# A fixed TensorE order around each layer norm in a ten-phase transformer kernel

## The chip, the cores and the metric

One core of a Trainium2 chip runs the whole program. The metric is device time in microseconds (us) from one launch; the runs shown are three, with their median.

## The reference

The input is 256 tokens of 1024 features in float32. Two blocks follow each other. What matters here is how a phase ends:

```python
# first block, i = 0, 1: windowed attention (i = 0) or a gated linear recurrence (i = 1), then an MLP
x = layer_norm(DN_ALPHA * x + (1.0 + gate) * y, ln_g[i, 0], ln_b[i, 0])
y = sq_relu_mlp(x * (1.0 + scale) + shift, mlp_w1[i], mlp_w2[i])
x = layer_norm(DN_ALPHA * x + (1.0 + gate) * y, ln_g[i, 1], ln_b[i, 1])
# second block, i = 0, 1: gated feed-forward, mixer (attention and a gated delta rule), gated feed-forward
x = layernorm(DN_ALPHA_2 * x + 0.5 * swiglu(x, ffn_w13[i, 0], ffn_w2[i, 0]), ln_g[i, 0], ln_b[i, 0])
x = layernorm(DN_ALPHA_2 * x + hybrid_mixer(x, ...), ln_g[i, 1], ln_b[i, 1])
x = layernorm(DN_ALPHA_2 * x + 0.5 * swiglu(x, ffn_w13[i, 1], ffn_w2[i, 1]), ln_g[i, 2], ln_b[i, 2])
```

Each layer norm takes a token's mean and variance over 1024 features and gives (x - mean) / sqrt(variance + 1e-5), times a row, plus a row. `shift`, `scale` and `gate` come from a small product with a condition vector. There are ten phases and so ten norms: attn, mlp0, rnn, mlp1, ffn00, mix0, ffn01, ffn10, mix1, ffn11.

## The kernel before

**Products.** All weights stream through SBUF once, as tiles of 128 x 1024, in the order of their use. `get` (L336) issues the loads on SyncE's queue and splits each tile exactly into a high part (`hi`, ScalarE, L356) and a low part (`lo`, VectorE, L360; in quarters of 256 columns around a norm). A product then takes three matmuls: hi with the input's high part, hi with its low part, lo with the high part (L384 to L386 for a projection up, L402 to L404 in `mv_mm` for a projection down). The residual X lies as two tiles, `X[0]` and `X[1]`, a half of the tokens (128) each over 1024 features. The next phase's input is wanted transposed, features down the partitions: `hT`, with a high part (ScalarE, L373) and a low part (VectorE, L375).

**The end of a phase.** A projection down accumulates in four PSUM banks, `acc[half, c]`, for two halves of the tokens and two halves of the columns. The last four weight tiles (`LAG`, the tail) are left to `finish` (L614), which goes through them a half of the tokens at a time: for each half and column half, four tiles with three matmuls each, 24 matmuls for a half of the tokens. Then `ln_stats` (L554) makes the half's norm: VectorE multiplies by the gate's row where there is one (L562), adds the residual (L565), makes statistics of each column half (L567) and joins them (L569); GpSimd adds the epsilon (L570) and takes the power -1/2 (L571). Where the next phase's input isn't modulated (`direct`: mlp1 and the six phases after it), VectorE applies mean and row (L574, twice) and the power and row (L576, twice). Elsewhere (attn, mlp0, rnn) VectorE makes one factor (L578) and ScalarE applies both (L580, twice), and the rows wait until the transpose.

**The next phase's first products.** `turn` (L582) transposes a half: TensorE makes eight transposes of 128 x 128 in two groups of four, one group per column half of X (L589), into two PSUM banks of the `acc` kind. The result is copied to `h32`, by two copies of ScalarE where the norm is direct (L591), else by eight instructions with the features' scale and shift, ScalarE and VectorE in turns (L598, L596). `head_mm` (L605) makes the products of the next phase's first three weight tiles (four for mlp0, rnn and mlp1) in plain float32 from `h32`, for that half alone: eight products a tile, each two instructions of TensorE in the trace (L612). `turn_split` (L601) makes the high and low part of `hT` for the half.

**What sets the order.** The kernel is written in a framework that gives each engine its list of instructions before the run: it goes through the program with simulated times, and on each engine takes among the instructions that are ready then the one that was written first, or one marked with a high priority (as `turn` is). TensorE's list at a norm so follows from those simulated times: transposes can come between down products, and head products in another order than the loops'. On the chip each engine works its list in order.

The tail of the attention phase is the output projection of its last four heads, 4 to 7. `ph_attn` (L664) interleaves the heads' scores, probabilities and values with these products; each head's values become a tile `tT` that the down product needs.

## Time and profile before

| | us |
|---|---|
| three runs | 2159.17, 2160.49, 2160.00 |
| median | 2160.0 |
| span of the profiled execution | 2157.3 |
| TensorE busy in it | 2074.2 |
| VectorE busy | 1496.5 |
| ScalarE busy | 1056.3 |
| GpSimd busy | 152.2 |

The span goes from the first to the last instruction of the one execution that the profiler took; a run's time also has what lies around it. PE is TensorE's matmul side, PEld its loading of stationary operands, DVE VectorE, ACT ScalarE, POOL GpSimd, SP SyncE. A line such as L404 is a line of the kernel. Matmuls overlap, and the end of one is modelled, so the start of the next tells more than the end. In brackets stand the idle time of an engine before an instruction, and what ended it.

### The profile page before, as it was taken

The page shows a single profiled execution, that of the slowest core. Times are in us where ns is not written, and L with a number is a line of the kernel's source. Part 1 is how long each engine was busy: PE and PEld are TensorE (multiplying, and loading weights), DVE is VectorE, ACT ScalarE, POOL GpSimd, SP SyncE. Part 2 cuts the span into 40 slices and gives each one's busy share as a digit, 9 for nine tenths or more (in the row PEclk, how much of TensorE's full clock was granted, in tenths as well). Part 3 has the DMA queues.
Part 4 walks back from the last instruction along what each step waited for, and adds up shares of the span by engine and source line. Part 5 has one row for each costly group of instructions (what it writes and reads, how often), then busy time and mean ns, then how long its engine had stood idle before and what let it go on. Part 6 is the DMA issues. An engine that isn't in the chain of part 4 may idle for free.

```text
span 2157.3 us, 36524 instructions
## 1 busy us (share of the span) xinstructions
PE 2074.2 (96%) x14806; PEld 1903.0 (88%) x14806; DVE 1496.5 (69%) x2522; ACT 1056.3 (49%) x1798; POOL 152.2 (7%) x178
## 2 busy tenths in 40 slices
PE   4879999999999999999999999999999999999997
PEld 4769999898898999988999899999999889998997
DVE  5788979987656655788966655565569886666555
ACT  2444445784444444466634444444436664444442
POOL 1110000001000000011011100000001100100000
PEclk9899999999999999999999999999999999999999
DMA  9758974454664655454424455555535433355552
GB/s 323 274 225 325 345 293 174 173 198 177 234 236 155 223 193 179 154 189 149 145 79 177 159 221 194 179 193 179 192 139 209 139 133 137 108 198 184 186 186 79
DMA packets 67832, 411.80 MB, mean 191 GB/s; under 512 B 8304, under 2 KB 8480, under 8 KB 26960
## 3 DMA queue, kind: packets, MB, share of 16 engines
q1 hardware_dynamic: 59904, 384.85, 48.9%
q0 software_dynamic: 7616, 24.45, 3.6%
q8 instruction: 116, 1.90, 0.4%
q14 instruction: 52, 0.43, 0.1%
q10 hardware_dynamic: 144, 0.18, 0.0%
HBM read 408.35 MB, written 4.24 MB: 191 GB/s over the span
## 4 chain that ended last, share of the span: by engine, by line
PE 77%; DVE 12%; ACT 5%; DMA 3%; issue 2%; POOL 2%; POOLq 0%; DVEq 0%; SPq 0%; ACTq 0%
PE pu L384 13%; PE pu L386 13%; PE pu L385 13%; PE acc L402 6%; PE acc L403 6%; PE acc L404 6%; PE hd L612 3%; DVE lo L360 3%; PE py L386 2%; PE py L384 1%; PE py L385 1%; ACT hi L356 1%; DMA raw<-wst 1%; DMA aw<-ada 1%; DVE X L565 1%
## 5 line engine op out<-in xcount | busy, mean ns | idle before, releaser
L360 DVE TENSOR_TENSOR lo<-raw,hi 128x1024 fp32r<-128x1024 f32 (+1 forms) x689 | 730.2, 1068 | 415.6 <-ACT hi L356 407.0
L356 ACT ACTIVATE hi<-raw 128x1024 fp32r<-128x1024 f32 x574 | 605.7, 1058 | 710.1 <-PE pu L385 350.5
L384 PE MATMUL pu<-hT,hi 128*128 128x256 f32 x2672 | 765.3, 286 | 0.0
L386 PE MATMUL pu<-hT,lo 128*128 128x256 f32 x2672 | 758.2, 284 | 2.4 <-DVE lo L360 2.4
L385 PE MATMUL pu<-hT,hi 128*128 128x256 f32 x2672 | 758.2, 284 | 0.0
L384 PEld LDWEIGHTS pu<-hT,hi 128*128 128x128 f32 x2672 | 512.1, 192 | 18.0 <-issue 10.9
L385 PEld LDWEIGHTS pu<-hT,hi 128*128 128x128 f32 x2672 | 512.1, 192 | 5.7 <-issue 0.3
L386 PEld LDWEIGHTS pu<-hT,lo 128*128 128x128 f32 x2672 | 511.9, 192 | 5.1 <-DVE lo L360 2.6
L402 PE MATMUL acc<-hi,tT 128*128 128x512 f32 x688 | 270.0, 395 | 2.6 <-ACT tT L373 2.5
L403 PE MATMUL acc<-hi,tT 128*128 128x512 f32 x688 | 270.5, 393 | 0.7 <-DVE tT L375 0.6
L404 PE MATMUL acc<-lo,tT 128*128 128x512 f32 x688 | 270.2, 393 | 0.0
L404 PEld LDWEIGHTS acc<-lo,tT 128*128 128x128 f32 x688 | 129.3, 188 | 28.0 <-DVE lo L360 0.4
L402 PEld LDWEIGHTS acc<-hi,tT 128*128 128x128 f32 x688 | 129.4, 188 | 27.5 <-ACT tT L373 3.6
L403 PEld LDWEIGHTS acc<-hi,tT 128*128 128x128 f32 x688 | 129.5, 188 | 24.5 <-DVE tT L375 1.9
L612 PE MATMUL hd<-h,raw 128*128 128x128 f32 x960 | 113.0, 277 | 0.1
L612 PEld LDWEIGHTS hd<-h,raw 128*128 128x128 f32 x960 | 110.6, 193 | 2.4 <-ACT h L591 1.5
L452 DVE SCALAR_TENSOR_TENSOR aacc<-aw,csil,aacc 128x1024 f32<-128x1024 f32 x70 | 89.5, 1278 | 1.7 <-DMA aw<-adaw 1.4
L570 POOL TENSOR_SCALAR mv<-mv 128x1 f32<-128x1 f32 x20 | 12.1, 607 | 1100.5 <-DVE mv L569 1100.5
L373 ACT ACTIVATE tT<-r 128x256 fp32r<-128x256 f32 x152 | 61.5, 405 | 39.9 <-DVE r L782 28.0
L807 DVE SCALAR_TENSOR_TENSOR r<-r,pu 128x256 f32<-128x256 f32 x84 | 35.4, 422 | 64.5 <-PE pu L386 64.4
L375 DVE TENSOR_TENSOR tT<-r,tT 128x256 fp32r<-128x256 f32 x152 | 64.1, 422 | 4.8 <-ACT tT L373 4.8
L1007 DVE SCALAR_TENSOR_TENSOR cv<-pu,cl,cv 128x255 f32<-128x255 f32 (+2 forms) x144 | 66.7, 472 | 0.3
(368 smaller groups left out, 2590.7 us busy)
## 6 DMA issues: line engine op xcount, KB each, us to landing
raw<-wst SPq DMA_DIRECT2D x318, 1024.0 KB, 4.9
aw<-adaw SPq DMA_DIRECT2D x80, 512.0 KB, 6.0
aw<-ada SPq DMA_DIRECT2D x16, 512.0 KB, 5.6
bias<-bias_d POOLq DMA_DIRECT2D x32, 192.0 KB, 2.7
g<-rows POOLq DMA_DIRECT2D x10, 512.0 KB, 4.2
b<-rows POOLq DMA_DIRECT2D x10, 512.0 KB, 5.2
bias_d<-ext_d POOLq DMA_DIRECT2D x1, 2048.0 KB, 18.9
gbc<-g_d POOLq DMA_DIRECT2D x4, 512.0 KB, 5.4
```

Source lines behind the costliest of these rows:

```text
L356: S.activation(out=hi[:, 0:n], in_=r, func=AF.Copy)
L360: V.tensor_tensor(out=lo[:, c:c + m], in0=r[:, c:c + m], in1=hi[:, c:c + m].bitcast(F32), op=ALU.subtract)
L375: (eng or V).tensor_tensor(out=dlo, in0=src, in1=dhi.bitcast(F32), op=ALU.subtract)
L384: T.matmul(ps, lhsT=hi[:, c], rhs=r[:, 0:256], start=kk == 0, stop=False)
L385: T.matmul(ps, lhsT=hi[:, c], rhs=r[:, 256:512], start=False, stop=False)
L386: T.matmul(ps, lhsT=lo[:, c], rhs=r[:, 0:256], start=False, stop=kk == KT - 1)
L402: T.matmul(ps, lhsT=th, rhs=hi, start=first, stop=False)
L403: T.matmul(ps, lhsT=tl, rhs=hi, start=False, stop=False)
L404: T.matmul(ps, lhsT=th, rhs=lo, start=False, stop=last)
L452: V.scalar_tensor_tensor(out=acc, in0=w, scalar=csil[:, k:k + 1], in1=acc, op0=ALU.mult, op1=ALU.add)
L612: T.matmul(ps[:, half * 128:half * 128 + 128], lhsT=w[:, kk * 128:kk * 128 + 128], rhs=h32[:, kk, :], start=kk == 0, stop=kk == KT - 1)
L1007: V.scalar_tensor_tensor(out=o[:, n:256], in0=ps[:, 0:256 - n], scalar=wc(3 - n), in1=o[:, n:256], op0=ALU.mult, op1=ALU.add)
```

## The change

Four things change, all in how a phase ends.

1. In `ln_stats` the epsilon is added by VectorE instead of GpSimd, and the function returns its last VectorE instruction of the half.
2. `finish` gives TensorE's instructions in a fixed order, that in which they are written (`manual_schedule` for TensorE alone; the other engines' lists are made as before). The order is: the first half's 24 down products; of the second half's eight units (a column half and a tile, three matmuls each) six, `n + 2`; the first half's eight transposes; the last two units; the first half's head products up to five before their end; the second half's transposes; the last five; the second half's head products. The last norm has no next phase, and only the order of its down products is fixed.
3. `head_mm` takes the place at which it calls for the transposes, and goes through tile after tile, with all eight products of a tile.
4. VectorE's part of the first half's `turn_split`, the low part of `hT`, is queued behind the last VectorE instruction of the second half's norm (`issue_after`).

Comments and docstrings are also taken out, which does nothing.

```diff
@@ -567,20 +567,21 @@
             V.bn_stats(out=stt[:, c, :], in_=X[half][:, s])
         mv = pool.tile([128, 3], F32, tag="mv", bufs=2, name="mv")
         V.bn_aggr(out=mv[:, 0:2], in_=stt)
-        G.tensor_scalar(out=mv[:, 1:2], in0=mv[:, 1:2], scalar1=1.0, scalar2=LN_EPS, op0=ALU.mult, op1=ALU.add)
+        V.tensor_scalar(out=mv[:, 1:2], in0=mv[:, 1:2], scalar1=LN_EPS, scalar2=None, op0=ALU.add)
         G.tensor_tensor(out=mv[:, 2:3], in0=mv[:, 1:2], in1=mhalf[:, 0:1], op=ALU.pow)
         if last:
             for s in cs_:
                 V.scalar_tensor_tensor(out=X[half][:, s], in0=X[half][:, s], scalar=mv[:, 0:1], in1=ln["g"][:, s], op0=ALU.subtract, op1=ALU.mult)
             for s in cs_:
-                V.scalar_tensor_tensor(out=X[half][:, s], in0=X[half][:, s], scalar=mv[:, 2:3], in1=ln["b"][:, s], op0=ALU.mult, op1=ALU.add)
-            return
-        V.scalar_tensor_tensor(out=mv[:, 1:2], in0=mv[:, 0:1], scalar=-1.0, in1=mv[:, 2:3], op0=ALU.mult, op1=ALU.mult)
+                ins = V.scalar_tensor_tensor(out=X[half][:, s], in0=X[half][:, s], scalar=mv[:, 2:3], in1=ln["b"][:, s], op0=ALU.mult, op1=ALU.add)
+            return ins
+        ins = V.scalar_tensor_tensor(out=mv[:, 1:2], in0=mv[:, 0:1], scalar=-1.0, in1=mv[:, 2:3], op0=ALU.mult, op1=ALU.mult)
         for s in cs_:
             S.activation(out=X[half][:, s], in_=X[half][:, s], func=AF.Identity, scale=mv[:, 2:3], bias=mv[:, 1:2])
+        return ins
 
     def turn(half):
-        """transpose a half of the normalised tokens, then the scale and shift of its features"""
+
         h32 = per.tile([128, KT, 128], F32, tag="b4", bufs=4, name="h32")
         for kq in range(2):
             pt = ps_acc("pt")
@@ -602,33 +603,54 @@
         h32 = state["h32", half]
         split(hT[:, :, half * 128:half * 128 + 128], hT[:, :, 256 + half * 128:384 + half * 128], h32)
 
-    def head_mm(half, keys, hps):
-        for n, key in enumerate(keys):
+    def head_mm(half, keys, hps, at=None, then=None):
+
+        n = 0
+        for key in keys:
             if half == 0:
                 hps[key] = (get(*key), ps_up("hd"))
             w, ps = hps[key]
-            h32 = state["h32", half]
             for kk in range(KT):
-                T.matmul(ps[:, half * 128:half * 128 + 128], lhsT=w[:, kk * 128:kk * 128 + 128], rhs=h32[:, kk, :], start=kk == 0, stop=kk == KT - 1)
+                if n == at:
+                    then()
+                n += 1
+                T.matmul(ps[:, half * 128:half * 128 + 128], lhsT=w[:, kk * 128:kk * 128 + 128], rhs=state["h32", half][:, kk, :],
+                         start=kk == 0, stop=kk == KT - 1)
 
     def finish(acc, tail, nxt):
-        """the last down products, a half of the tokens at a time, the norm, and the next phase's first products"""
+
+
         n = len(tail)
         keys = [(nxt,) + it for it in items_of(nxt)[:nf(nxt)]] if nxt else []
         hps = {}
         if nxt:
             hT = per.tile([128, KT, 512], F32R, tag="hT", bufs=1, name="hT")
-        for half in range(2):
-            for c in range(2):
-                for j, (t, (hi, lo)) in enumerate(tail):
-                    mv_mm(acc[half, c], t, half, hi[:, c * 512:c * 512 + 512], lo[:, c * 512:c * 512 + 512], False, j == n - 1)
-            ln_stats(half, acc, ln["direct"])
+
+        def turn_(half):
+            with tc.high_priority():
+                turn(half)
+
+        def down(half, units):
+            for c, j in units:
+                t, (hi, lo) = tail[j]
+                mv_mm(acc[half, c], t, half, hi[:, c * 512:c * 512 + 512], lo[:, c * 512:c * 512 + 512], False, j == n - 1)
+
+        units = [(c, j) for c in range(2) for j in range(n)]
+        with tc.manual_schedule(engines={mybir.EngineType.PE}):
+            down(0, units)
+            ln_stats(0, acc, ln["direct"])
+            down(1, units[:n + 2])
+            if nxt:
+                turn_(0)
+            down(1, units[n + 2:])
+            ins = ln_stats(1, acc, ln["direct"])
+            if nxt:
+                head_mm(0, keys, hps, 8 * len(keys) - 5, lambda: turn_(1))
+                with tc.issue_after(ins.ins):
+                    turn_split(0, hT)
+                head_mm(1, keys, hps)
+                turn_split(1, hT)
         if nxt:
-            for half in range(2):
-                with tc.high_priority():
-                    turn(half)
-                head_mm(half, keys, hps)
-                turn_split(half, hT)
             for key in keys:
                 head[key] = hps[key][1][:, 0:256]
             state["hT"] = hT
@@ -640,7 +662,7 @@
         ln["es"].close()
```

## Rows read from the trace of the kernel before

**Rows 1.** The page's first part: each engine's busy time in the span.
```profile
PE 2074.2 (96%) x14806; PEld 1903.0 (88%) x14806; DVE 1496.5 (69%) x2522; ACT 1056.3 (49%) x1798; POOL 152.2 (7%) x178
```
**Rows 2.** Waits of PE at the transposes: us in total, times, longest us.
```profile
PE pt L589 <- ACT X L580: 7.5, 5, 5.3
PE pt L589 <- DVE X L576: 6.3, 12, 0.6
```
**Rows 3.** Timeline of PE, end of ffn00 (start, us, engine, line, operation [idle before]).
```profile
890.29 0.39 PE L402 MATMUL acc<-hi,tT 128*128 128x512 f32 x1
890.52 0.39 PE L403 MATMUL acc<-hi,tT 128*128 128x512 f32 x1
891.47 0.66 PE L589 MATMUL pt<-cs,X 128*128 128x128 f32 x4 [0.56 <-DVE X L576]
```
**Rows 4.** Down products behind the transposes: stretch, PE busy (count); mlp0, rnn, mlp1, ffn00.
```profile
343.70:344.85 1.15, 0.92 (x3) 1.00 0.00 0
512.80:513.45 0.65, 0.38 (x1) 1.00 0.00 0
700.70:701.20 0.50, 0.50 (x2) 1.00 0.00 0
891.95:894.02 2.07, 1.88 (x7) 1.00 0.00 0
```
**Rows 5.** Timeline of DVE and POOL, end of ffn00, first half's norm.
```profile
887.09 0.69 DVE L565 SCALAR_TENSOR_TENSOR X<-X,acc 128x512 f32<-128x512 f32 x1 [0.28 <-PE acc L404]
...
888.54 0.21 DVE L569 BATCH_NORM_AGGREGATE mv<-stt 128x2 f32<-128x12 f32 x1
888.79 1.41 DVE L574 SCALAR_TENSOR_TENSOR X<-X,mv,g 128x512 f32<-128x512 f32 x2
890.66 1.42 DVE L576 SCALAR_TENSOR_TENSOR X<-X,mv,b 128x512 f32<-128x512 f32 x2 [0.46 <-POOL mv L571]
...
889.67 0.95 POOL L571 TENSOR_TENSOR mv<-mv,mhalf 128x1 f32<-128x1 f32 x1
```
**Rows 6.** The epsilon on POOL, all norms: duration ns min/median/max, first and last start.
```profile
L570 POOL TENSOR_SCALAR mv<-mv x20: 183/742/1287, 147.6 to 2148.5; 128x1 f32<-128x1 f32 x20
```
**Rows 7.** Timeline of DVE and PE, end of ffn00, second half's norm.
```profile
895.77 1.21 DVE L375 TENSOR_TENSOR hT<-h,hT 128x1024 fp32r<-128x1024 f32 x1
...
899.89 0.63 PE L589 MATMUL pt<-cs,X 128*128 128x128 f32 x4 [0.56 <-DVE X L576]
...
901.21 0.60 PE L612 MATMUL hd<-h,raw 128*128 128x128 f32 x3
```
**Rows 8.** Timeline of PE, both halves' transposes at mlp0's, rnn's and mlp1's end.
```profile
343.21 0.66 PE L589 MATMUL pt<-cs,X 128*128 128x128 f32 x4 [0.46 <-ACT X L580]
...
352.66 1.36 PE L589 MATMUL pt<-cs,X 128*128 128x128 f32 x8 [0.45 <-ACT X L580]
...
512.30 0.65 PE L589 MATMUL pt<-cs,X 128*128 128x128 f32 x4 [0.79 <-ACT X L580]
...
518.72 0.66 PE L589 MATMUL pt<-cs,X 128*128 128x128 f32 x4 [0.49 <-ACT X L580]
...
699.58 1.32 PE L589 MATMUL pt<-cs,X 128*128 128x128 f32 x8 [0.37 <-DVE X L576]
...
707.23 1.38 PE L589 MATMUL pt<-cs,X 128*128 128x128 f32 x8 [0.50 <-DVE X L576]
```
**Rows 9.** Timeline of DVE, rnn's end: the last scaled features of the second half.
```profile
522.34 0.76 DVE L596 TENSOR_SCALAR h<-pt,ha,hb 128x128 f32<-128x128 f32 x2
```
**Rows 10.** Attention's norm: transposes; stretches with PE busy (count), granted clock, DMA share, GB/s.
```profile
149.55 1.97 PE L589 MATMUL pt<-cs,X 128*128 128x128 f32 x8 [5.31 <-ACT X L580]
...
141.15:144.25 3.10, 3.08 (x13) 1.00 0.95 390
149.50:153.00 3.50, 3.45 (x16) 0.50 0.00 0
153.00:167.60 14.60, 14.60 (x131) 1.00 0.68 247
```

## The prediction

> **What bounds the kernel now.** I read the page's first part: of the span's 2157.3 us TensorE is busy for 96% [rows 1]. So a change of TensorE's order can only win what TensorE idles away around the norms, and the waits of TensorE say how much that is: its transposes waited 7.5 us for ScalarE's normalised rows and 6.3 us for VectorE's, 17 waits in all [rows 2]. One of the 17 is 5.3 us, at the norm after the attention; the other 16 make 8.5 us. A wait is longer on TensorE's clock than the idle time shown: a product lasts 0.39 us but the next starts 0.23 us after it [rows 3], so each wait also loses the 0.16 us in which its predecessor drains. Outside the attention that is 8.5 + 16 × 0.16 = 11.1 us, half a per cent of the time: **the ceiling** of this change, but for the attention's norm and the last norm's end.
>
> The execution in the profile has a span of 2157.3 us; the median of the timed runs is 2160.0, 2.7 us more, which holds what lies around the span. I carry every sum over to the median. A measurement of this kernel can tell some 0.2%, 4.3 us, from no change.
>
> **Five plain norms (ends of ffn00, mix0, ffn01, ffn10, mix1).** I work one, ffn00's, and the others repeat its pattern.
>
> First half. The transposes start at 891.47, where the products before them would have let them start at 890.52 + 0.23: 0.72 us lost [rows 3]. Seven of the second half's 24 down products stood behind the transposes' start [rows 4], 17 ahead. The change puts 18 ahead (6 units of 3): nearly the order that there is. The extra product covers 0.23 us. The other help is the epsilon, which goes from GpSimd to VectorE. The chain on VectorE is residual sum 887.09, aggregate 888.54, L574 twice, then L576, which waits for GpSimd's power [rows 5]. The power ends at 889.67 + 0.95 = 890.62 and L576 starts 0.04 later, while L574 was done at 888.79 + 1.41 = 890.20. GpSimd's epsilon takes 0.74 us in the median and 0.18 at the least [rows 6]. On VectorE I take 0.2 us, by the aggregate's 0.21 us, the nearest row of a tiny VectorE instruction; bounds are 0.1 and 0.4. Then L574 ends at 890.4, the power before that, and L576 starts at 890.45 instead of 890.66: 0.2 us won. Against this, the four later transposes need the second column half of X, which comes 0.71 us (half of L576's 1.42) after the first, while four transposes take 0.45: 0.26 us of new wait, where before a down product filled it. First half: 0.23 + 0.2 − 0.26, **0.2 us won**.
>
> Second half. Its transposes start at 899.89 with 0.56 + 0.16 = 0.72 us lost; the head products behind them start at 901.21 [rows 7], 1.32 us after 899.89, which is 0.2 more than the ten instructions between (0.113 us each) need: 0.9 in all. In VectorE's chain stands the low part of the first half's input (L375), 1.21 us from 895.77 [rows 7]. The change holds it back behind the norm: 1.1 us off the chain (0.1 overlapped). With 0.2 for the epsilon and 0.2 for down products that end sooner, X is ready for TensorE at about 898.4. But TensorE's order moves too: the transposes come after 19 of 24 head products instead of 23. Head products start at about 893.8; one is two instructions of 0.113 us (131 instructions, eight of them transposes, in 14.6 us [rows 10]), so 19 take 4.3 us: TensorE is there at 898.1. That leaves 0.3 us of wait and 0.26 for the second column half, against 0.9: **0.35 us won**. The five products that are left (1.1 us) cover the copies. L375 itself costs nothing where it goes: VectorE has nothing from 900.4 but the next weights' low parts, and the low part is wanted only when the head products end, after 905. If that cover went, the price would be its 1.21 us.
>
> Five norms × (0.2 + 0.35) = **2.7 us won**.
>
> **Four norms with a gate.** Here the order does move, by the counts of [rows 4]: 3 products stood behind the transposes at mlp0's end, 1 at rnn's, 2 at mlp1's; now 6. So the transposes come up 3, 5 and 4 products sooner (0.7, 1.1 and 0.9 us) and X comes only 0.2 us sooner: first halves lose 0.5, 1.0 and 0.7 us, and rnn's another 0.3 for the second column half, which a product covered. Second halves lost 0.61 (mlp0), 0.65 (rnn) and 0.66 (mlp1) [rows 8], and 0.3 more between the two groups at mlp0 and mlp1 (eight transposes take 1.36 and 1.38 us where 1.06 would do). Without L375, mlp0's second half wins its 0.9 whole; mlp1's chain had no L375 in it, wins 0.1. At rnn I expect 0.15: fixed order runs a tile's eight head products through all features before the next tile, and the last of rnn's scaled features ended at 522.34 + 0.76 = 523.1, 4.4 us after its transposes began [rows 8, 9], where 5 products, 8 transposes and 7 products of a tile cover 3.6. Sum: mlp0 +0.4, rnn −1.15, mlp1 −0.6: **1.3 us lost**.
>
> The attention's norm. At 141.18 TensorE gets head 7's values and needs 12 more products in 3.1 us (13 instructions with the last of an earlier one) [rows 10]; the other tail products had filled gaps earlier. In fixed order (column half by column half, all four tiles in each), only three products each of heads 4, 5 and 6 can run early. So 39 products, 9.0 us, stand behind 141.2, 33 of them ahead of the transposes. They fill the hole of 5.31 us before 149.55 [rows 10] and the first half's sum starts later: its last columns come at about 145.7 (15 products, 0.4 to drain, and an estimated 0.6 for head 7's low part), 4.3 us of chain (887.09 to 891.47), transposes at 150.0 plus 0.3. Six products and the eight transposes later, at 152.6, the head products start, 1.3 us later than now. [...] I take **1.0 us lost**; bounds are 1.7 won (only the clock's gain counts) and 7.9 lost (the rival "attention").
>
> The last norm has no transposes; the epsilon saves its 0.2 us on the path to the end. No DMA is added or moved past; GpSimd's queue loses 20 short instructions. TensorE's other queue neighbours keep their place, since all that follows needs the new input.
>
> **Sum:** 2.7 − 1.3 − 1.0 + 0.2 = 0.6 us won. The framework will also order the other engines anew; no row prices that, and I add nothing for it to the sum (to the range some 2 us on either side). So 2160.0 − 0.6 = 2159.4 us.
>
> [...] The rows show that GpSimd and VectorE get into each other's way: 0.18 us alone, 0.74 beside L574 [rows 5, 6], and the power ended 0.43 us after the second L574. [...] But GpSimd's epsilon had ended before the power began at 889.67, while the second L574 ran until 890.20 [rows 5], so I take it that the power can slip in between the two as well. Otherwise it is the rival "port".
>
> **The rivals.**
> *Hidden* (faster): second halves wait no more, because VectorE's chain tightens by more than I allow once L375 is out. For it: L375 is the one long piece between stats and aggregate. Against: 4 products fewer are ahead of the transposes. It wins 0.55 more at five norms, 0.85 at mlp1, 0.5 at rnn: 4.1 us, so 2155.3, and with 1.0 at the attention, if the held clock pays for the delay there, 2154.3; its limit, all 11.1 us, is 2149.
> *Attention* (slower): TensorE, emptied of 27 tail products before 141.2, idles there as long as before 149.55, its clock falls to the 0.50 level in front of the 39 products, and 27 × 0.23 = 6.2 us plus 1.7 us at half clock stand uncovered. For it: the clock did fall once, after 5.31 us. Against: the scores and probabilities of heads 6 and 7 stay there to break the idle time, and the norm's own chain was waited out anyway. It decides where an idle stretch before 141.2 grows as long as that of 5.31 us. Instead of 1.0 lost, 7.9: 2159.4 + 6.9 = 2166.3.
> *Port*: at 13 chains (two halves of six norms with L574, the last) the power ends 0.43 us after both L574s: 0.17 us later than now instead of 0.2 sooner, 13 × 0.37 = 4.8: 2164.2.
> *Nothing moves*: the framework's order was 17 products against 18; if the fixed order is otherwise the same, only the epsilon counts, 0.2 us where the transposes wait for it and at the end, some 2 us: 2158.
>
> **How the numbers follow.** Forecast 0.48, hidden 0.25, attention 0.13, port 0.08, nothing moves 0.06. The forecast's own range is 2156 to 2162. The range goes from 2152 (into hidden, short of its limit) to 2164.5 (past port, short of attention), leaving out some 0.2. Faster than 2155.7 is hidden, 0.25; slower than 2164.3 is attention, 0.13; the rest, 0.62, is within 0.2%.
>
> **What would show it.** In the changed profile: the plain norms' transposes waiting some 0.3 us twice in each half; L375 of the first half behind L576; the power starting right after a VectorE epsilon, and ending before L574 (else port); rnn's and mlp1's first transposes waiting over 1.2 us; at the attention, no hole of 5 us and a granted clock of 1.00 to 155 us. Second halves with no wait mean hidden; a clock of 0.50 before 145 us means attention. The forecast is wrong if the head products end more than 3 us sooner or later against the norm's start than the sums say, or if the difference arises between norms.

## The result and the profile after

| | before | changed |
|---|---|---|
| timed runs, median (lowest to highest), us | 2159.59 (2158.43 to 2160.49) | 2170.4 (2168.54 to 2174.82) |
| span of the profiled execution, us | 2157.3 | 2167.8 |

The changed kernel is **slower**: the ratio of its runs to those of the kernel before is 1.0064, with a 95% interval of 1.005 to 1.0078. The prediction was 2159.4 us with a range of 2152 to 2164.5, so it was wrong. (The ratio on record is not the quotient of the two medians, which is 1.005.)

The page's first part, against [rows 1]:

```profile
PE 2083.8 (96%) x14806; PEld 1908.8 (88%) x14806; DVE 1499.8 (69%) x2542; ACT 1060.7 (49%) x1798; POOL 142.1 (7%) x158
```

TensorE has the same 14806 instructions and the same share of the span, but they take 9.6 us more. Most of that, 7.2 us, is at the attention's norm, where part of them ran at a lower clock (stretches below). Next TensorE's waits, in the columns of [rows 2] (us in total, times, longest us):

```profile
PE pt L590 <- ACT X L580: 10.5, 5, 3.5
...
PE pt L590 <- DVE X L576: 1.8, 2, 1.2
```

The transposes are now at L590. Their waits for VectorE's rows, at the direct norms, have nearly gone (12 waits and 6.3 us before, 2 and 1.8 now). Their waits for ScalarE's rows, at the three norms with scaled features, have grown from 7.5 to 10.5 us. The total at the transposes is even a little lower, 12.3 against 13.8, so this view alone doesn't explain 10 us.

What does is to ask where along the program the two executions come apart. I compared the start of the same product up (the k-th hi-times-high-part product in both traces) ahead of each norm and behind it. The table says how many us later each kernel is behind the norm than the kernel before, counted from ahead of it, in one profiled execution each. At the attention I count from the last instruction that stands at the same place in every kernel's list of TensorE (at 124.24 us in the kernel before). Up to there the lists are the same, and yet the other executions come there 2.7 to 5.8 us sooner: the kernel before was slow there in its profiled execution, which is no effect of any edit. The plain norms are five, summed. Kernels with the same edits at a norm differ there by up to 1.5 us (2 at e2's plain norms), so smaller differences between two cells say little.

| kernel | attn | mlp0 | rnn | mlp1 | plain norms | whole span |
|---|---|---|---|---|---|---|
| changed | +12.7 | +3.9 | +1.3 | +0.6 | −4.7 | +10.5 |
| e1, attention in the framework's order | +1.5 | +3.4 | +1.3 | +0.6 | −5.0 | −0.4 |
| e2, fixed at the plain norms only | +2.9 | +0.1 | −1.8 | −0.4 | −2.8 | −7.3 |
| e3, epsilon on GpSimd | +12.4 | +2.1 | +2.3 | +1.6 | +0.2 | +17.6 |
| e4, low part free | +13.6 | +2.9 | −0.3 | +3.3 | +0.1 | +13.6 |
| e5, attention tile by tile | +5.4 | +3.9 | +1.3 | +0.7 | −4.6 | +4.4 |
| e6, none left behind at mlp0, rnn | +11.3 | +1.3 | −0.4 | +0.6 | −5.2 | +1.6 |
| e7, next phase's work tied | +6.8 | +2.3 | −0.2 | +0.7 | −4.9 | +3.3 |
| e8, two VectorE edits, no order | +3.2 | −1.0 | −1.8 | −0.5 | −6.4 | −8.5 |
| e9, epsilon alone | +2.1 | +0.2 | −0.5 | −0.4 | −1.1 | −4.8 |
| e10, low part alone | +0.1 | +0.3 | −1.4 | −0.1 | +1.2 | +2.4 |
| e11, order mended | +0.8 | +2.8 | +3.4 | +0.6 | −5.0 | −1.6 |
| e12, e8 and next phase's work tied | +0.1 | −0.8 | −0.7 | −0.5 | −6.4 | −6.8 |

The rest of each span's difference lies ahead of the attention's norm, between norms (the framework also orders the other engines anew) and at the last norm. So the change won 4.7 us at the plain norms, and lost 18.5 at the four norms of the first block, 12.7 of it at the attention's. Together that is 13.8 us lost (the last norm, where 1.1 us are won, is not in the table); the ratio of 1.0064 is 13.8 us as well.

The attention's part as a whole, from the common instruction to the first product up behind the norm, before and then changed (stretch, PE busy (count), granted clock, DMA share, GB/s):

```profile
124.24:170.18 45.94, 38.48 (x243) 0.93 0.63 240
```

```profile
121.12:179.76 58.64, 45.65 (x243) 0.85 0.73 260
```

**The attention's norm.** First the kernel before, then the changed one, in stretches of 4 us (the changed execution is 3.1 us ahead at the common instruction):

```profile
132.00:136.00 4.00, 2.64 (x13) 1.00 0.60 240
136.00:140.00 4.00, 3.21 (x16) 1.00 0.29 51
140.00:144.00 4.00, 3.99 (x18) 1.00 0.96 396
```

```profile
132.00:136.00 4.00, 1.44 (x5) 1.00 0.01 2
136.00:140.00 4.00, 2.77 (x9) 0.75 0.83 275
140.00:144.00 4.00, 4.00 (x10) 0.50 0.98 397
144.00:148.00 4.00, 4.00 (x17) 0.89 0.69 249
```

Between 132 and 140 us TensorE ran 29 instructions before (28 in the 8 us that are the same place of the program), and 14 now; the down products that had filled the gaps stand, in their fixed order, behind products of heads whose values aren't there. Its granted clock falls to 0.50, at which ten products then run one behind the other. TensorE's timeline of the changed kernel (start, us, engine, line, operation [idle before]) shows what follows:

```profile
139.64 0.79 PE L402 MATMUL acc<-hi,tT 128*128 128x512 f32 x1 [0.47 <-ACT tT L373]
...
145.39 0.39 PE L404 MATMUL acc<-lo,tT 128*128 128x512 f32 x1
...
152.82 1.36 PE L590 MATMUL pt<-cs,X 128*128 128x128 f32 x8 [2.84 <-ACT X L580]
...
155.43 0.83 PE L617 MATMUL hd<-h,raw 128*128 128x128 f32 x6
...
165.95 1.97 PE L590 MATMUL pt<-cs,X 128*128 128x128 f32 x8 [3.47 <-ACT X L580]
...
179.76 0.28 PE L384 MATMUL pu<-hT,hi 128*128 128x256 f32 x1
```

The product at 145.39 is the first half's last. The first transposes come 3.3 us later than before [rows 10], 6.4 us later at the same place of the program, and the second ones wait a second time, 3.47 us. In the kernel before the second half's chain had begun in the one hole (at 146.69 us) and ended under the first head products, and its transposes came at 154.03 without a wait. At 165.95 the clock is low once more (0.61 from 165.95 to 169.50 us). The first product up, at 170.18 before, comes at 179.76.

VectorE's timeline shows what kept the second half. Its own links are L562, L565, L567, L569, L570 and L578:

```profile
157.04 0.68 DVE L562 TENSOR_TENSOR t<-acc,g 128x512 f32<-128x512 f32 x1
157.64 0.75 DVE L450 TENSOR_SCALAR aacc<-aw,csil 128x1024 f32<-128x1024 f32 x1
158.30 0.69 DVE L565 SCALAR_TENSOR_TENSOR X<-X,t 128x512 f32<-128x512 f32 x1
158.90 1.28 DVE L452 SCALAR_TENSOR_TENSOR aacc<-aw,csil,aacc 128x1024 f32<-128x1024 f32 x1
160.09 0.69 DVE L567 BATCH_NORM_STATS2 stt<-X 128x6 f32<-128x512 f32 x1
160.75 1.23 DVE L360 TENSOR_TENSOR lo<-raw,hi 128x1024 fp32r<-128x1024 f32 x1
161.89 0.20 DVE L569 BATCH_NORM_AGGREGATE mv<-stt 128x2 f32<-128x12 f32 x1
162.01 1.17 DVE L360 TENSOR_TENSOR lo<-raw,hi 128x1024 fp32r<-128x1024 f32 x1
163.10 0.15 DVE L570 TENSOR_SCALAR mv<-mv 128x1 f32<-128x1 f32 x1
163.16 1.28 DVE L452 SCALAR_TENSOR_TENSOR aacc<-aw,csil,aacc 128x1024 f32<-128x1024 f32 x1
164.89 0.16 DVE L578 SCALAR_TENSOR_TENSOR mv<-mv 128x1 f32<-128x1 f32 x1 [0.45 <-POOL mv L571]
```

VectorE is never idle but for the last 0.45 us, and yet the chain takes 8.0 us. The framework has put an instruction of the mlp0 phase into every gap of it: multiply-adds of the modulation (L450, L452) and full-width low parts of weights (L360). Where nothing is put into such a gap it is short (0.03 us between L569 and L570 at ffn00's norm, second half, in this kernel), and the work in it here is 0.75 to 1.28 us long.

### The profile page after: what moved, and what is told of

It is laid out like the page before. It is cut to its first block, busy times and chain, and to the rows that moved or that the text cites. A ratio compares the mean times of both kernels' runs of the same rounds, so it can differ in the third digit from the quotient of the medians.

```text
span 2167.8 us, 36514 instructions
## 1 busy us (share of the span) xinstructions
PE 2083.8 (96%) x14806; PEld 1908.8 (88%) x14806; DVE 1499.8 (69%) x2542; ACT 1060.7 (49%) x1798; POOL 142.1 (7%) x158
## 5 line engine op out<-in xcount | busy, mean ns | idle before, releaser
L360 DVE TENSOR_TENSOR lo<-raw,hi 128x1024 fp32r<-128x1024 f32 (+1 forms) x689 | 730.6, 1069 | 415.8 <-ACT hi L356 406.8
L571 POOL TENSOR_TENSOR mv<-mv,mhalf 128x1 f32<-128x1 f32 x20 | 19.4, 972 | 1121.0 <-DVE mv L570 1121.0
L452 DVE SCALAR_TENSOR_TENSOR aacc<-aw,csil,aacc 128x1024 f32<-128x1024 f32 x70 | 89.4, 1277 | 2.6 <-DMA aw<-adaw 2.3
L375 DVE TENSOR_TENSOR tT<-r,tT 128x256 fp32r<-128x256 f32 x152 | 64.1, 422 | 5.3 <-ACT tT L373 5.3
```

Source lines behind the costliest of these rows:

```text
L360: V.tensor_tensor(out=lo[:, c:c + m], in0=r[:, c:c + m], in1=hi[:, c:c + m].bitcast(F32), op=ALU.subtract)
L375: (eng or V).tensor_tensor(out=dlo, in0=src, in1=dhi.bitcast(F32), op=ALU.subtract)
L452: V.scalar_tensor_tensor(out=acc, in0=w, scalar=csil[:, k:k + 1], in1=acc, op0=ALU.mult, op1=ALU.add)
```

## Experiments

The kernel before ran beside each of them on the same chip, with medians between 2155 and 2157 us there, so what counts is the ratio; where an expectation is in microseconds, I set beside it the ratio times the 2159.6 us of the kernel before. (By that rule the changed kernel is at 2173.4, and not at the 2170.4 from which the expectations count.) In the expectations "the planner" is the part of the framework that makes the engines' lists, and P, S, E, L, H, F, B, T, P', O and F' are theories.

### Is it the place of the order, or something else?

```diff
 e1, e2: finish()
+        if ph not in FIXED:      # e1: all but attn; e2: the ffn and mixer phases
+            for half in range(2):
+                down(half, units)
+                ln_stats(half, acc, ln["direct"])
+            for half in range(2 if nxt else 0):
+                turn_(half)
+                head_mm(half, keys, hps)
+                turn_split(half, hT)
 e3: ln_stats()
-        V.tensor_scalar(out=mv[:, 1:2], in0=mv[:, 1:2], scalar1=LN_EPS, ...
+        G.tensor_scalar(out=mv[:, 1:2], in0=mv[:, 1:2], scalar1=1.0, scalar2=LN_EPS, ...
 e4: finish()
-                with tc.issue_after(ins.ins):
-                    turn_split(0, hT)
+                turn_split(0, hT)
```

> The changed kernel with the order at the attention norm alone left to the planner, as before the change; everything else as changed. Theory P (the fixed order pays at the plain norms and costs at the attention norm, where TensorE is held to products whose values are late, and at the norms of mlp0 and rnn): the 9.6 us by which the two traces come apart at the attention norm come back, 2160 to 2162 us, and TensorE waits for X before its first transposes about 5 us, not 6.3. Rival S (the losses come from the planner's other choices, that any edit stirs, not from the order at this norm): within 3 us of the changed kernel's 2170.4. Rival E (the epsilon on VectorE): no change either, 2170.

> The fixed order at the norms of the ffn and mixer phases and at the end alone (six of ten); at attn, mlp0, rnn and mlp1 the planner's order as before. Theory P: the five plain norms win 0.9 us each and the end 1.1, together about 5.7 on the kernel before, so 2153 to 2156 us, less than both kernels. Rival S: between 2159 and 2168, since the mixers' other work is stirred again. Rival E (epsilon on VectorE at all ten norms is what costs): 2165 to 2170.

> The changed kernel with the epsilon's addition back on GpSimd. Theory P: the order is the cause, the addition a small gain of the change, so 2170 to 2173 us. Rival E (one more step of VectorE's chain, ahead of which the planner sets other work of up to 1.3 us): some 3 to 8 us faster, 2162 to 2167.

> The changed kernel without the tie of the first low part to the second half's norm. Theory P: the tie is worth nothing much, 2168 to 2173 us. Rival L (the tie makes the first up products of the next phase late, by the low part's 1.3 us at each of nine norms): 2159 to 2165.

| | median, us | ratio to before | 95% interval |
|---|---|---|---|
| e1 | 2159.6 | 1.0016 | 1.0003 to 1.003 |
| e2 | 2151.95 | 0.9981 | 0.9965 to 0.9998 |
| e3 | 2174.73 | 1.0079 | 1.0059 to 1.0099 |
| e4 | 2177.55 | 1.0095 | 1.0076 to 1.0114 |

The order at the attention's norm alone costs 0.5% (1.0064 against 1.0016). (e1 also leaves the low part untied at this norm; e4, untied with the order kept, loses as much there as the changed kernel, so the tie is not the cause.) With the order taken away at mlp0, rnn and mlp1 too, the kernel is faster than before. Against the 2159.6 us that is 2163.1 and 2155.5: P's second number came, and its first was missed by 1 us; the first transposes of e1 wait 6.0 us, and not about 5. But only half of P holds: e3 and e4 say that the gain of the plain norms comes from somewhere else. Take either of the two edits of VectorE away, keep the whole order, and the plain norms win nothing (+0.2 and +0.1 in the table). E and L, by which these runs would have been faster, are ruled out by the times. That each of the two edits helps is seen in the table; by time, e3's interval overlaps widely with the changed kernel's and e4's barely. P had taken both edits for nearly free: 1.0079 and 1.0095 are 2176.7 and 2180.1 us, above its ranges.

(In e2 the plain norms win 2.8 us and not 4.7, because of ffn10's norm alone, which loses 1.2; its cause is told with e9 and e10.)

What the two edits do is seen in VectorE's timeline at ffn00's norm, second half. In the changed kernel:

```profile
908.75 0.68 DVE L565 SCALAR_TENSOR_TENSOR X<-X,acc 128x512 f32<-128x512 f32 x1
...
912.63 0.21 DVE L569 BATCH_NORM_AGGREGATE mv<-stt 128x2 f32<-128x12 f32 x1
912.87 0.15 DVE L570 TENSOR_SCALAR mv<-mv 128x1 f32<-128x1 f32 x1
912.94 1.41 DVE L574 SCALAR_TENSOR_TENSOR X<-X,mv,g 128x512 f32<-128x512 f32 x2
914.26 1.41 DVE L576 SCALAR_TENSOR_TENSOR X<-X,mv,b 128x512 f32<-128x512 f32 x2
915.59 1.22 DVE L375 TENSOR_TENSOR hT<-h,hT 128x1024 fp32r<-128x1024 f32 x1
```

With the epsilon on GpSimd (e3) L576 waits for the power, as before:

```profile
908.91 0.68 DVE L565 SCALAR_TENSOR_TENSOR X<-X,acc 128x512 f32<-128x512 f32 x1
...
914.90 1.41 DVE L576 SCALAR_TENSOR_TENSOR X<-X,mv,b 128x512 f32<-128x512 f32 x2 [0.44 <-POOL mv L571]
```

With the low part free (e4) it stands in the chain again, as in [rows 7]:

```profile
906.29 0.68 DVE L565 SCALAR_TENSOR_TENSOR X<-X,acc 128x512 f32<-128x512 f32 x1
...
910.06 1.21 DVE L375 TENSOR_TENSOR hT<-h,hT 128x1024 fp32r<-128x1024 f32 x1
...
912.81 1.41 DVE L576 SCALAR_TENSOR_TENSOR X<-X,mv,b 128x512 f32<-128x512 f32 x2
```

From the first L565 to the end of L576 that is 6.92 us in the changed kernel, 7.41 without the epsilon's move and 7.93 without the tie; in the kernel before, 8.42. The two steps, 0.5 and 1.0 us, simply add up.

### What loses at the first block's norms

e5 gives the attention's last products another fixed order, e6 leaves no products behind the first transposes at mlp0 and rnn, e7 keeps the next phase's VectorE work out of the attention's norm, and e8 has the two VectorE edits without any order.

```diff
 e5: finish(), for ph == "attn"
+                for half in range(2):
+                    down(half, [(c, j) for j in range(n - 2) for c in range(2)])
+                units = [(c, j) for j in range(n - 2, n) for c in range(2)]
             down(0, units)
             ln_stats(0, acc, ln["direct"])
-            down(1, units[:n + 2])
+            down(1, units[:2])
 e6: finish(), for mlp0 and rnn
-            down(1, units[:n + 2])
+            down(1, units)
             turn_(0)
-            down(1, units[n + 2:])
 e7: behind() is issue_after(the last VectorE instruction of the attention's norm) during mlp0
+                    with behind():
                         ada_mac(*seq[n - 3])
+                with behind() if m == n else ExitStack():
                     for c in range(0, n, m):
                         V.tensor_tensor(out=lo[:, c:c + m], ...
 e8: FIXED = (), and in the order as written
+                ins = ln_stats(half, acc, ln["direct"])
                 head_mm(half, keys, hps)
+                with tc.issue_after(ins.ins):
                     turn_split(half, hT)
```

> The changed kernel, with the last down products of the attention phase alone in another fixed order: both halves and both column halves of heads 4 and 5 first, then heads 6 and 7; the transposes have the same 6 products behind them. Theory H (at this norm the fixed order holds some 30 ready products behind head 7's values, so TensorE stands idle between 132 and 140 us at a falling clock, and the first half's last product ends at 147.2 us instead of about 143): 4 to 6 us faster than the changed kernel, 2164 to 2166, and the granted clock is 1.00 between 140 and 144 us. Rival F (the norm's links on VectorE set the end, with work of the next phase between them): within 2 us, 2168.5 to 2171.

> The changed kernel with the first transposes behind all of the second half's products at the norms of mlp0 and rnn (none left behind them, where the change leaves 6). Theory B (the transposes stand 1.8 and 2.1 us in front of 6 products that were ready): the waits shrink by the 6 x 0.233 = 1.4 us at each, 2 to 3 us faster, 2167 to 2168. Rival (the second half's chain, which starts 1.4 us earlier then, has its own wait of the same length later, or was late for another reason): 0 to 5 us faster, with the gain in the second transposes' wait too. Rival F (the chain of VectorE decides, not the place of the transposes): within 1 us of 2170.

> The changed kernel; VectorE's work of the mlp0 phase that needs no norm (the modulation's multiply-adds, 0.74 and 1.28 us, and the full-width low parts of weight tiles, 1.22 us) is tied behind the attention norm's second half. Theory F (between the links of the second half's chain, 157.04 to 165.05 us, 4.5 us of such work stand, and two more multiply-adds in the first half's): the second transposes start 4 us earlier or more, 2164 to 2167 us. Rival H (the held tail products alone): within 2 us of 2170. If the tied work is then missing later: 2170 to 2174, with waits for the low parts in mlp0.

> The kernel before with the change's two edits of VectorE alone (the epsilon on VectorE, the first low part behind the second half's norm), and the planner's order on TensorE at every norm. Theory P (the order itself is what wins at the plain norms): a ratio to before between 0.9990 and 1.0010. Rival T (those two edits make the gain of the plain norms, and the order only costs): a ratio of 0.9965 to 0.9985, as fast as with the order fixed at the plain norms or faster.

| | median, us | ratio to before | 95% interval |
|---|---|---|---|
| e5 | 2161.66 | 1.0031 | 1.0019 to 1.0043 |
| e6 | 2166.05 | 1.0058 | 1.0044 to 1.0072 |
| e7 | 2167.59 | 1.006 | 1.0042 to 1.0079 |
| e8 | 2150.77 | 0.9983 | 0.9971 to 0.9995 |

**e5** is clear by its time: its interval lies wholly below that of the changed kernel, and the attention's part of the table falls from +12.7 to +5.4. H said 4 to 6 us faster than the changed kernel, 2164 to 2166; the two ratios are 7.1 us apart (2166.3 against 2173.4), and at the place itself the gain is 7.3. The granted clock is 1.00 from 140 to 144 us, as H said, but no product runs there. (H's 147.2 us is a misreading: the first half's last product ended at 145.39 + 0.39 = 145.78.) Its profile shows the tail in the gaps again (stretches, as above), and what is left over, in TensorE's timeline:

```profile
136.00:140.00 4.00, 3.33 (x12) 1.00 0.96 396
140.00:144.00 4.00, 0.00 (x0) 1.00 0.60 243
144.00:148.00 4.00, 3.44 (x12) 0.57 0.40 137
```

```profile
144.56 1.97 PE L591 MATMUL pt<-cs,X 128*128 128x128 f32 x8 [4.59 <-ACT X L581]
...
157.51 1.82 PE L591 MATMUL pt<-cs,X 128*128 128x128 f32 x8 [2.85 <-ACT X L581]
```

The first transposes are 8.3 us earlier than in the changed kernel, 7.2 at the same place of the program. But TensorE stood idle for 4.59 us in front of them with six products ready behind them, and the second half's norm could begin only after those six. Its chain ended late, and the second transposes wait 2.85 us. An order with no product left behind the first transposes was tried at mlp0 and rnn (e6), not here.

**e7**: by time no difference from the changed kernel can be told (the intervals overlap almost wholly, and 1.006 gives 2172.6 us, 0.9 less than the changed kernel, where F's 2164 to 2167 are 3 to 6 less). So F is not shown by time. The third outcome, tied work that is missing later, isn't either: between the norms of attn and mlp0 TensorE has no wait for a low part. In the trace, which is of the fastest of e7's six runs (2162.43 us), F does hold: the attention's part falls from +12.7 to +6.8. In the first half the transposes come 4.4 us after its last product's end, where the changed kernel has 7.0 (145.78 to 152.82). VectorE's timeline of the second half, from its first link, L568, to its last, L584 (a quarter of a weight's low part, L362, is the longest other piece that is left in it, beside scaled features):

```profile
151.89 0.68 DVE L568 TENSOR_TENSOR t<-acc,g 128x512 f32<-128x512 f32 x1
...
154.77 0.41 DVE L362 TENSOR_TENSOR lo<-raw,hi 128x256 fp32r<-128x256 f32 x1
...
156.15 0.16 DVE L584 SCALAR_TENSOR_TENSOR mv<-mv 128x1 f32<-128x1 f32 x1 [0.67 <-POOL mv L577]
```

The chain takes 4.4 us instead of 8.0, and the second transposes start at 158.49 without any wait. By the table e5 gives back 7.3 us of the 12.7 and e7 5.9. (The expectation of e11 counts otherwise: 8.4 and 7.6 from the program's start, and 13.9 from the last product up ahead of the norm.)

**e6**: timed, its gain over the changed kernel (0.06%) is smaller than the intervals. At the two norms the trace, which is of the fastest of its six runs (2160.55 us), shows 2.6 and 1.7 us less. That is more than the 1.4 us that six products last, as the first rival to B has it: the second transposes wait less as well, and at rnn, where the changed kernel's granted clock is 0.71 from 525 to 530 us and the six products behind the first wait of 1.96 us take 2.6 us, e6 waits for X only once, 0.6 us. The waits of TensorE at mlp0's norm, in the changed kernel and then in e6:

```profile
PE pt L590 <- ACT X L580: 2.2, 2, 1.6
...
PE acc L403 <- DVE tT L375: 0.6, 1, 0.6
```

```profile
PE pt L591 <- ACT X L581: 0.2, 1, 0.2
PE acc L404 <- DVE tT L376: 0.2, 1, 0.2
```

**e8** settles what the gain was. With no fixed order anywhere it is faster than before by 0.17%, as fast as e2. The ratio is in T's range, though the upper end of its interval reaches into P's; the table decides between them. Theory P, by which the order wins at the plain norms, falls; T stands. The framework, given the same two edits, makes nearly the same order at a plain norm by itself: 18 down products ahead of the first transposes, six behind them. The five plain norms win 6.4 us in this kernel, 1.7 more than in the changed one. So the order was worth nothing there, and it costs at four other norms.

### One edit alone, and both ways on

```diff
 e9: the kernel before, with
-        G.tensor_scalar(out=mv[:, 1:2], in0=mv[:, 1:2], scalar1=1.0, scalar2=LN_EPS, ...
+        V.tensor_scalar(out=mv[:, 1:2], in0=mv[:, 1:2], scalar1=LN_EPS, ...
 e10: the kernel before, with
+                with tc.issue_after(ins.ins):
                     turn_split(half, hT)
 e11: the changed kernel, with e5's edit at attn, e6's at mlp0 and rnn, e7's at attn and mlp0
 e12: e8, with e7's edit at attn, mlp0 and rnn
```

> The kernel before with the epsilon on VectorE alone. Theory T (the two edits of VectorE each shorten the second half's chain at a plain norm: 8.42 us before, 7.93 in the run with the epsilon on VectorE and the low part free, 7.41 the other way round, 6.92 with both): a chain of 7.9 us at ffn00's norm, some 0.4 us won at each of five plain norms, a ratio of 0.9985 to 1.000. Rival (only the two together win, since the low part covers GpSimd's time): no gain, 1.000 or above.

> The kernel before with the first low part tied behind the second half's norm alone. Theory T: a chain of 7.4 us at ffn00's norm, some 0.9 us won at each plain norm, a ratio of 0.998 to 0.9995. Rival (only the two together win): no gain, 1.000 or above.

> The changed kernel with its order on TensorE kept but mended where it lost: the attention phase's last products tile by tile, no product left behind the first transposes at mlp0 and rnn, VectorE's work of the next phase tied behind the norm at attn and mlp0. Theory P' (a fixed order costs by what it puts in a late place, not by being fixed): the runs before gave back 8.4 us and 7.6 us of the 13.9 at the attention norm, which overlap, and 2.6 and 1.7 at mlp0 and rnn, so 2152 to 2158, a ratio of 0.998 to 1.001. Rival O (a fixed order loses against the planner's in itself): above 1.002.

> The planner's order on TensorE with the epsilon on VectorE, the low part tied, and the next phase's VectorE work tied behind the norms of attn, mlp0 and rnn too. Theory F' (such work between the links costs in the planner's order as well): a ratio of 0.996 to 0.998, below the 0.9983 of the same kernel without the last tie. Rival (there the chain is interleaved with the other half and covered, and the tied work is missing later): 0.9983 to 1.001.

| | median, us | ratio to before | 95% interval |
|---|---|---|---|
| e9 | 2155.44 | 0.9993 | 0.9978 to 1.0007 |
| e10 | 2157.04 | 1.0002 | 0.9989 to 1.0015 |
| e11 | 2161.52 | 1.0012 | 0.9999 to 1.0026 |
| e12 | 2148.01 | 0.9959 | 0.9942 to 0.9975 |

**e9 and e10**: the chain at ffn00's norm takes 7.92 and 7.39 us (T's 7.9 and 7.4). But neither time can be told from before. e10's ratio is what the rival said, and e9's fits both. In the traces the rival doesn't hold. At mix0's, ffn01's and mix1's norms each edit alone wins: 1.0 to 1.1 us with the epsilon on VectorE, 0.4 with the low part tied, and 1.3 to 1.4 with both (e8). With the epsilon alone the framework already leaves six products behind the first transposes, and no transposes wait at these three norms; with the low part alone it leaves seven, as before, and they wait 0.4 to 0.6 us in each half.

At ffn00's and ffn10's norms, the two with a mixer phase behind them, both runs lose (0.3 us each at ffn00's; 1.7 and 2.1 at ffn10's). ScalarE's list is made anew too. In e9 and e10 it has the load of a table for the mixer's first activation ahead of both copies of the second transposes, and the head products wait, 1.3 us in e9 and 0.4 in e10. In the kernel before and in e8 the load stands between the two copies, and no head product waits for it. At ffn00's norm in e9 (ScalarE, then TensorE):

```profile
896.91 1.28 ACT L1014 ACT_TABLE_LOAD   x1 [5.46 <-DVE X L577]
...
898.94 5.62 PE L618 MATMUL hd<-h,raw 128*128 128x128 f32 x48 [1.32 <-ACT h L593]
```

The rest of ffn10's loss is a weight tile whose load landed late. Its high part waited 2.2 us for it in e9, 2.7 in e10 and 3.0 in e2 (0.4 before), and in each of them the first half's chain and transposes were late by it (the transposes wait 1.2, 2.4 and 1.9 us).

So each edit wins time by itself where nothing else comes in its way. With TensorE's order fixed (e3, e4) only both together do.

**e11** lies between its two theories (0.998 to 1.001, or above 1.002), and its interval reaches into both. The mending takes back most of what the order lost, and the attention's part is as good as in the framework's order (+0.8, and +1.5 in e1). At mlp0 and rnn it still loses 2.8 and 3.4 us. Its waits over the whole run have two kinds that before had not at these norms, head products that wait for VectorE's scaled features, and tail products for their tiles' parts:

```profile
PE hd L624 <- DVE h L604: 3.6, 7, 0.9
PE acc L405 <- ACT tT L376: 2.3, 3, 1.3
```

At mlp0 the first kind makes 2.0 us, at rnn the second 1.3. Whether the tile-by-tile order or the tied work makes them was not tried apart.

**e12** is the fastest: 0.41% below the kernel before, and its interval doesn't reach 0.998. The ratio, 0.9959, lies at the edge of what F' said and outside the rival's range. But its interval overlaps that of e8 (0.9971 to 0.9995), so what the last tie adds is not settled, and the mechanism of F' is not shown: in e8's chains at the three norms only one large piece of such work was left to move (a multiply-add of 1.28 us at mlp0's, second half), and mlp0's part of the table is about the same in both (−1.0 and −0.8). The two together, the epsilon on VectorE and ties that keep unneeded VectorE work behind the norm, without any order on TensorE, are the version to keep.

## Why the prediction was wrong

**The plain norms: direction right, cause right, size too small.** 2.7 us were forecast, 4.7 came (6.4 without the order). The low part and the epsilon were named as the two helps, and the timeline confirms both as they stood in the working: L375 out of the chain 1.0 us (1.1 forecast), the epsilon 0.5 (0.2 forecast; on VectorE it delays L574 by 0.07 us, not 0.2, and L576 now follows L574 at once, so the whole idle time in front of it went). What the working subtracted, second column halves coming late and four fewer products ahead of the second transposes, hardly shows: there "hidden" came true. The last norm's 0.2 was 1.1: so much less lies between the last product up and the end of the span, here and in the other runs with the epsilon on VectorE, and nothing less in the two without (e3, e10). The two halves' chains stand one behind the other on VectorE there, and each lost its wait for the power (0.46 and 0.44 us).

**The four norms with a gate: the sign held, the size didn't, and at mlp0 not even the sign.** Forecast +0.4 at mlp0, −1.15 at rnn and −0.6 at mlp1 (won or lost); measured −3.9, −1.3 and −0.6. mlp1's is right. rnn's is right in its sum, partly by luck: the second transposes no longer wait at all (0.5 us won, 0.15 forecast), and a fall of the clock behind the first wait, which was not in the working, took that back (granted clock 0.71 from 525 to 530 us; in the kernel before it was 1.00 from 505 to 525). At mlp0 three things were missed. The six products behind the transposes were priced by how much sooner the transposes come up, 0.5 us; but they also hold up the second half's chain, and e6 prices the whole at 2.6 (0.7 of it in the tail, below). The second half was to win 0.9 without L375; but a multiply-add of 1.27 us for a later phase (L452) stood in its place in the chain, and the second transposes and the head products behind them waited 0.63 and 0.67 us. And the timeline shows 0.91 us of idle time in the tail itself (0.33 for a tile's high part, 0.58 for its low part); as e6, with the same order in the tail, idles 0.2 us there, that is not the order alone:

```profile
344.13 0.50 PE L402 MATMUL acc<-hi,tT 128*128 128x512 f32 x1 [0.33 <-ACT tT L373]
345.21 0.50 PE L403 MATMUL acc<-hi,tT 128*128 128x512 f32 x1 [0.58 <-DVE tT L375]
...
354.42 1.36 PE L590 MATMUL pt<-cs,X 128*128 128x128 f32 x8 [1.60 <-ACT X L580]
```

**The attention's norm: this is the step that failed.** "I take 1.0 us lost", with a bound of 7.9; 12.7 came (11.2 against e1). The count was right: 39 products stand behind head 7's values, 33 of them ahead of the transposes. That the first half's last product ended at 145.78 us (145.7 forecast) is luck: at the common instruction this execution was 3.1 us ahead, so at the same place of the program it was 3.2 us late. Three things were not in the sum.

First, the clock. The 1.0 and the bound of 1.7 won count on a clock that holds over this norm, which no run shows: in the changed kernel it was 1.00 from 148 to 164 us, but 0.50 from 140 to 144 and 0.61 from 165.95 to 169.50, and over the attention's part 0.85 where before it was 0.93. The products held back left TensorE idle before 140 us (1.44 of 4 us busy from 132 to 136), and the clock fell to 0.50 before the 39 began (0.50 from 138.2 to 139.64 us); the first 15 took 6.1 us (139.64 to 145.78) where the working had 4.5, and head 7's values came later too. It is the rival "attention", to which I gave 0.13, and its sign came (0.50 before 145 us). My reason against it (the scores and probabilities break the idle time) was wrong: they leave 14 instructions in 8 us, and the clock fell with no single wait there longer than 2.02 us.

Second, VectorE. The chain was priced with the 4.3 us of ffn00, whose gaps hold small pieces, and here larger work of the next phase stood in it: from the first half's last product to its transposes it took 7.0 us where the working had 4.6 (4.4 in e7, which keeps that work out). So the head products started 4.1 us later than before by the clock and 7.2 at the same place, not 1.3: at 155.43, where 152.6 was forecast.

Third, and largest, I followed only the first half. Before, the second half's chain ran in the hole and under the first head products; in the fixed order it comes after the first transposes and six products, takes 8.0 us, and ends in a wait of its own of 3.47 us and a second fall of the clock. The remaining 5.5 us of the 12.7 were lost there, where the sum had stopped, and the rival's 7.9 was too small for the same reason.

**Of the rivals**, "port" didn't come: the power took a median of 1.00 us beside L574, ended before the second L574 did (by 0.3 us in ffn00's second half), and L576 waits for nothing. "Nothing moves" was right about the plain norms' order in a way I hadn't seen: the framework itself arrives at that order once the epsilon is on VectorE (e8, e9).

## What to carry to other kernels

A fixed order on an engine that works its list in order (in e5 TensorE idled 4.59 us with six ready products behind the transposes that it waited for) is a claim about when every operand arrives; check it at each place it applies to, and let no ready work stand behind an operand that is known to come late, above all not work that starts the next dependent chain. Where a change both fixes an order and shortens a chain, try the chain alone first: here it was all of the gain. Try each edit alone too, and then look at the lists of all engines, as the framework makes them anew. When a short dependent chain runs on a shared engine, look at what fills the gaps between its links; work that nobody needs yet belongs behind the chain's last link.

## What the runs showed of the hardware

In e5 the clock's fall was paid behind the gap, not in it: the granted clock was 1.00 from 140 to 144 us with no product at all, and the next 4 us, with 12 instructions, had 0.57. So that hole was dearer than its idle time, by what the next products took at the lower clock. In the changed kernel, at 0.50 from 140 to 144 us, it was 0.43 us from one tail product to the next, where 0.23 is usual.

GpSimd's power took 0.56 us with VectorE idle beside it (e7, attention's norm, second half), 1.00 in the median of the changed kernel's 14 beside L574, and 1.53 beside a multiply-add of 1.28 us, after whose end it came to its own end 0.4 us later:

```profile
163.33 1.53 POOL L571 TENSOR_TENSOR mv<-mv,mhalf 128x1 f32<-128x1 f32 x1 [11.61 <-DVE mv L570]
```

In the kernel before, GpSimd's epsilon likewise took 0.18 us with VectorE idle (rnn's norm, second half) and 1.29 beside such a multiply-add (mlp0's, second half). What makes GpSimd's instructions longer beside VectorE's was not shown. Beside the two L574 of the second half at ffn00's norm, in the changed kernel, the power ended 0.4 us after the first and 0.3 before the second, so it didn't wait out both. The 1.53 us are a second price of other work between the links: L578 waits 0.45 us for the power after L452 has ended.
